# Both heads in one step of a windowed attention, uncast indices and unscaled queries in a routing, and another queue for the gates: one change in four places

## The chip, the cores and the metric

The kernel runs on one core of a Trainium2 chip. The metric is device time in microseconds of one execution; every comparison is between medians of several runs. The engines are TensorE (PE, its weight loads PEld), VectorE (DVE), ScalarE (ACT), GpSimd (POOL) and SyncE (SP, which here issues transfers only).

## The reference

Two transformer-like blocks over 512 tokens of 1024 numbers, in float32, then a norm. The change lies in the second block, which computes (cut):

```
h  = rmsnorm(x);  z = h @ w_in + b_in
conv = silu(layernorm(causal_conv31(val * sigmoid(gate)))) @ w_conv_out
# attention: 16 query heads, 2 key heads, window of 128 keys, one sink per head
m  = maximum(max(s), sink);  e = exp(s - m)
p  = e / (sum(e) + exp(sink - m));  attn = (p @ v) @ w_attn_o
x  = x + (sigmoid(g_conv) * conv + sigmoid(g_attn) * attn) @ w_out
# experts
h2 = rmsnorm(x)
q  = (h2 @ w_pq) in 8 heads of 2 halves;  sc = q . sub_keys      # 128 keys a half
s_top, i_top = top16(sc)                  # for each half
best, pos    = top16(s_top0[:, None] + s_top1[None, :])
idx  = i_top0 * 128 + i_top1 at pos;  gate = softmax(best)       # 128 experts a token
out  = sum over them of gate * gelu(u[idx] . h2) * v[idx]
```

The first block has a stick-breaking attention, a chunked attention, a short convolution and a gated feed-forward part; it is touched by nothing here.

## The kernel before, in words

Features lie on partitions, tokens along the row. Weights come as "units" of 128x1024 numbers, two to a transfer of 1 MB on SP (tile `raw`, two buffers). ScalarE rounds a unit to a high half (`w183h` for unit 183), VectorE or POOL takes the rest as a low half (`w183l`); there are three buffers of each. A product is then three matrix products: high by low, low by high, high by high. `linear` runs a unit's 24 of them into one PSUM tile.

Everything else is a side generator. `Merge` holds lanes (`at` attention, `cv` and `cg` convolution, `ln` norms, `ls` routing, `rw` rows), each with a width, the number of its generators that run at a time. `Clock` models when each engine is free, from sizes only (`cost`): on VectorE 960 elements a microsecond and partition, twice that if all operands are bf16. Ahead of each step of the main stream the generators whose due time has come by the model's TensorE time emit their next step. So a changed modelled cost moves instructions on all engines. `yield ("ls",)` in the main stream runs a lane to its end first.

The stages that matter here, in the order of time:

- Second block's input units with the attention beside them (`swa`, line 865). A generator takes one tile of queries, two heads. It runs four rounds (two pairs of query blocks by two heads): scores into PSUM tiles `w`, their maximum, three operations on the small tile `m` on VectorE, exponentials on ScalarE (`p`), transposes (`pt`), a copy (`pT`), products with the values (`o`), and a multiply by the reciprocal (`oq`).
- The convolution's statistics (`mu`), the layer norm, and its output product `co`.
- Queries of the routing (`pq`), multiplied by the norm's factor (`pqs`), scores (`sk`, copied to `skc`), and `top16` of each 128 (`head_lists`, 16 of them); then for each block of 128 tokens the candidates and their indices (`block_best`), where a one-hot `eq` picks the index.
- 128 units of u (w180 to w307, `u{o}{j}` is unit 180 + 8o + j). Every product of tokens 128 to 511 with all experts is formed, and gelu on ScalarE gives `last`, the activations. For the first 128 tokens rows of u and v are fetched by indirect transfers from POOL (`row`, `last`; four buffers) and VectorE takes the products (a custom instruction, printed as ISA in the order).
- Beside these, for token blocks 1 to 3, `gates`: the chosen indices and gates are transposed (`ijg`, `ijb`); for every 8 tokens VectorE makes five one-hot tiles (`hot`), TensorE multiplies them (`gp`, 24 products of 128x128), ScalarE copies them out (`stage`), and a transfer writes them to `g_dr`. In names such as `hot_3120` the first digit behind `hot` is which of the five, the next the block, the rest the token.
- Behind u15_3 (w303) the lane of the routing is drained and `last_phase` opens new buffers and fetches the gates of the first group of experts (`goct`); behind u15_7 the v units follow (w308 on): `wv` = activation by gate, and products `acc`.

Of the kernel before, what the change touches and what calls it, by code (L numbers as in the profile page):

```python
# [21 lines left out]
P = 128  # L22
# [168 lines left out]
def body(tc, a):  # L191
# [5 lines left out]
    with ExitStack() as ctx:  # L197
# [126 lines left out]
        def t2(name, dt=F32):  # L324
            return wk.tile([P, T], dt, tag="t2", name=name, bufs=NT2)
# [539 lines left out]
        def swa(i):  # L865
            q, k = q2[i], kt2[0]
            oq = t2(f"oq{i}")
            for n, (pr, e) in enumerate(((0, 0), (0, 1), (1, 0), (1, 1))):
                head = 2 * i + e
                if e == 0:  # L870

                    scs = [psd(f"w{i}{n}{x}") for x in range(2)]
                    for sc in scs:
                        PE.matmul(sc, identb, band[:, pr], start=True, stop=False, skip_group_check=True)
                    for b in range(2):
                        qb = 2 * pr + b
                        k0 = max(qb - 1, 0) * P
                        for x, sc in enumerate(scs):
                            rows = slice(x * 64, x * 64 + 64)
                            PE.matmul(sc[:, b * 256 + (P if qb == 0 else 0):(b + 1) * 256],  # L880
                                      q[rows, qb * P:(qb + 1) * P], k[rows, k0:(qb + 1) * P], start=False, stop=True,
                                      skip_group_check=True)
                    sc = None
                sv = scs[e].rearrange("p (b k) -> p b k", b=2)
                scs[e] = None
                m = wk.tile([P, 6, 2], F32, tag="m2", name=f"m2{i}{n}", bufs=8)
                sink = nsk[:, head:head + 1].to_broadcast([P, 2])
                V.tensor_reduce(m[:, 0], sv, axis=AX.X, op=ALU.max, negate=True)

                V.scalar_tensor_tensor(m[:, 1], m[:, 0], 0.125, sink, ALU.mult, ALU.min)  # L890
                V.tensor_tensor(m[:, 2], m[:, 1], sink, ALU.subtract)
                S.activation(m[:, 3], m[:, 2], AF.Exp)
                s = t2(f"p{i}{n}")
                for b in range(2):
                    S.activation(s[:, b * 256:b * 256 + 256], sv[:, b], AF.Exp, scale=0.125, bias=m[:, 1, b:b + 1],
                                 accum_out=m[:, 4, b:b + 1])
                sv = None
                yield at(s)
                V.tensor_tensor(m[:, 5], m[:, 3], m[:, 4], ALU.add)
                V.reciprocal(m[:, 5], m[:, 5])  # L900
                pt = psd(f"pt2{i}{n}")
                c0 = P if pr == 0 else 0
                for c in range(c0 // P, 4):
                    PE.transpose(pt[:, c * P:(c + 1) * P], s[:, c * P:(c + 1) * P], ident)
                pT = t2(f"pT2{i}{n}")
                if e:
                    S.activation(pT[:, c0:], pt[:, c0:], AF.Copy)
                else:
                    V.tensor_copy(pT[:, c0:], pt[:, c0:])
                yield at(pT)  # L910
                o = psd(f"o2{i}{n}")
                for b in range(2):
                    qb = 2 * pr + b
                    cs_ = [c for c in range(2) if qb - 1 + c >= 0]
                    for c in cs_:
                        PE.matmul(o[:, b * 64:(b + 1) * 64], pT[:, (2 * b + c) * P:(2 * b + c + 1) * P],
                                  v2[qb - 1 + c][:, e * 64:(e + 1) * 64], start=c == cs_[0], stop=c == 1)
                V.tensor_tensor(oq.rearrange("p (b e d) -> p b e d", b=NB, e=2)[:, 2 * pr:2 * pr + 2, e],
                                o[:, :P].rearrange("p (b d) -> p b d", b=2),
                                m[:, 5][:, :, None].to_broadcast([P, 2, 64]), ALU.mult)  # L920
# [168 lines left out]
        iota = wk.tile([P, P], F32, name="iota")  # L1089
# [10 lines left out]
        V.tensor_copy(iota16, iota[:, 0:16, None].to_broadcast([P, 16, 16]))  # L1100

# [40 lines left out]
        def block_best(b):  # L1142
# [15 lines left out]
            S.activation(best[:, 1], best[:, 1], AF.Exp)  # L1158
# [5 lines left out]
            far = wk.tile([P, 8, 16], F32, tag="far", name=f"far{b}", bufs=1)  # L1164
            V.tensor_scalar(far, pos[:, 0], float(NC1), None, ALU.is_ge)
# [3 lines left out]
            V.tensor_tensor(d, d, far[:, None].to_broadcast([P, 2, 8, 16]), ALU.mult)  # L1169
# [89 lines left out]
        def peer_u():  # L1259
            mg.spawn("ln", rms_steps(acc, "n4", rr))  # L1260
            for h in range(8):
                qs = []
                for c in range(2):
                    o = yield from linear(hp, f"pq{h}{c}")
                    if h + c == 0:
                        yield ("ln",)
                        mg.spawn("ln", norm2())
                    t = t2(f"pqs{h}{c}")
                    V.tensor_tensor(t, o, rr[1], ALU.mult)
                    qs.append(t)  # L1270
                mg.spawn("ls", head_lists(h, qs))
# [31 lines left out]
        def last_phase():  # L1303
# [8 lines left out]
            h2t.append(wk.tile([P, D], F32, name="h2s"))  # L1312
            S.activation(h2t[1], h2tok, AF.Copy)
            del h2t[0]
            fetch_g(0)

        def fetch_g(n, quarters=range(4)):
            for q in quarters if n < NOCT else ():
# [3 lines left out]
                nc.sync.dma_start(octs[n][:, c], g_dr[VORD[n]][:, c])  # L1322
# [218 lines left out]
```

## Time and profile before

| | |
|---|---|
| median of 3 runs | 2441.09 us (2439.46 to 2441.44) |
| profiled execution | 2439.86 us |
| its span | 2437.8 us |
| mean granted clock of TensorE | 0.988 |
| TensorE, VectorE, ScalarE, POOL busy | 97%, 72%, 42%, 30% |

All compute instructions pass through one helper (line 134), so tiles and not lines tell what an instruction is. The profile leaves out the numbers of tiles in one line's group, so `m` stands for all small tiles of the attention. A row's busy time adds overlapping matrix products once. What an engine waits for is the last releaser of that wait.

### The profile page before, as it was taken

Reading aid. Unit: us, or ns where it says so; the run is one execution under the profiler, and the core shown is the slowest. Engines: PE = TensorE matmul, PEld = TensorE weight load, DVE = VectorE, ACT = ScalarE, POOL = GpSimd, SP = SyncE. Lnnn points to the kernel's source line nnn. Section 1 sums busy time; section 2 is a strip of 40 time slices with the busy share of each in tenths; the row PEclk is TensorE's granted clock in tenths of the full one; section 3 lists DMA queues with packets and bytes.
Section 4 is the critical chain, followed back from the end, with each engine's and each line's share of the span. In section 5 each row is a group of like instructions: output and inputs, shape, how many; then the busy total and the mean of one; then the engine's idle time right before and its main releaser. Section 6 shows DMA issues by size and latency. Waiting matters only on the chain.

```text
span 2437.8 us, 33926 instructions
## 1 busy us (share of the span) xinstructions
PE 2364.7 (97%) x13114; PEld 2111.2 (87%) x13121; DVE 1759.3 (72%) x3167; ACT 1036.0 (42%) x1558; POOL 741.0 (30%) x586
## 2 busy tenths in 40 slices
PE   9999999999999889999999999999998999999997
PEld 7777888888776667777889999999997999999997
DVE  4637644443357789755789898999996888888874
ACT  4454433232246456444324334455554333333333
POOL 2122011110126578401233455333322332323211
PEclk9999999999999999999999999999999999999998
DMA  4110222222211112222224788899998999999972
GB/s 169 57 54 35 91 97 93 104 87 104 87 67 55 52 53 87 87 87 91 93 94 173 292 316 301 313 327 347 345 323 265 360 359 364 353 362 355 372 292 85
DMA packets 141857, 466.14 MB, mean 191 GB/s; under 512 B 10624, under 2 KB 61952, under 8 KB 112000
## 3 DMA queue, kind: packets, MB, share of 16 engines
q1 hardware_dynamic: 52416, 281.04, 31.5%
q0 software_dynamic: 36864, 134.23, 15.5%
q10 hardware_dynamic: 52416, 48.70, 5.9%
q8 instruction: 103, 1.69, 0.3%
q14 instruction: 58, 0.48, 0.1%
HBM read 414.65 MB, written 49.28 MB: 190 GB/s over the span
## 4 chain that ended last, share of the span: by engine, by line
PE 66%; issue 14%; DVE 10%; POOL 4%; ACT 3%; DMA 2%; SPq 0%; POOLq 0%; DVEq 0%; ACTq 0%
PE acc L134 22%; PE u L134 9%; PE up L134 5%; PE gate L134 5%; PE pq L134 3%; PE wo L134 2%; PE qkb L134 2%; DVE hot L134 2%; PE co L134 2%; PE gc L134 2%; POOL row L1054 1%; POOL last L1054 1%; PE ga L134 1%; PE ao L134 1%; DVE cyp L134 1%
## 5 line engine op out<-in xcount | busy, mean ns | idle before, releaser
L134 POOL TENSOR_TENSOR cy<-cy,cvt 128x511 f32<-128x511 f32 (+14 forms) x120 | 173.5, 1445 | 69.7 <-ACT cvt L134 59.1
L134 ACT ACTIVATE last<-u 128x384 f32<-128x384 f32 x128 | 63.0, 492 | 226.1 <-PE u L134 225.9
L1054 POOL DMA_INDIRECT last<-in_un,eid x64 | 80.5, 1257 | 167.9 <-DVE ea L134 131.4
L1054 POOL DMA_INDIRECT last<-in_vn,eid x64 | 70.8, 1106 | 198.9 <-DVE yt L134 188.6
L1054 POOL DMA_INDIRECT row<-in_un,eid x64 | 82.3, 1285 | 136.4 <-DVE ea L134 133.5
L1054 POOL DMA_INDIRECT row<-in_vn,eid x64 | 74.1, 1158 | 153.5 <-DVE yt L134 143.6
L134 ACT ACTIVATE stage<-gp 128x512 f32<-128x512 f32 x96 | 95.9, 1110 | 8.0 <-PE gp L134 8.0
L134 DVE TENSOR_TENSOR hot<-hot,ijb 128x1024 bf16<-128x1024 bf16 x144 | 91.0, 686 | 1.5
L134 PE MATMUL gp<-hot,hot 128*128 128x128 bf16 x1152 | 76.0, 221 | 14.1 <-ACT last L134 6.7
L134 PEld LDWEIGHTS <-hot 128*128 128x128 bf16 x1152 | 67.5, 98 | 24.0 <-DVE hot L134 19.6
L134 DVE SCALAR_TENSOR_TENSOR cyp<-u,par,cyp 128x511 f32<-128x511 f32 (+28 forms) x116 | 85.3, 735 | 2.4
L134 DVE CUSTOM_DVE_ANT_0 last<-last,h2tok 128x1024 f32<-128x1024 f32 x64 | 77.2, 1212 | 10.6 <-DMA last<-in_un,eid 10.6
L134 DVE SCALAR_TENSOR_TENSOR yt<-last,ea,yt 128x1024 f32<-128x1024 f32 x63 | 80.5, 1278 | 2.1 <-DMA last<-in_vn,eid 2.1
L134 DVE SCALAR_TENSOR_TENSOR yt<-row,ea,yt 128x1024 f32<-128x1024 f32 x64 | 81.8, 1278 | 0.1
L134 DVE CUSTOM_DVE_ANT_0 row<-row,h2tok 128x1024 f32<-128x1024 f32 x64 | 77.2, 1213 | 5.7 <-DMA row<-in_un,eid 5.3
L134 ACT ACTIVATE cvt<-u,par 128x511 f32<-128x511 f32 (+14 forms) x120 | 78.9, 700 | 0.0
L134 DVE TENSOR_TENSOR wv<-last,goct 128x384 f32<-128x384 f32 x128 | 70.5, 551 | 0.0
L134 DVE TENSOR_TENSOR hot<-iota,ijb 128x1024 bf16<-128x1024 bf16 x96 | 61.7, 683 | 0.0
L134 DVE TENSOR_TENSOR su<-up,n2r 128x512 f32<-128x512 f32 x22 | 15.2, 691 | 51.8 <-PE up L134 51.8
L134 PEld LDWEIGHTS o<-v,pT 128*128 128x128 f32 x224 | 29.6, 199 | 18.4 <-DVE pT L134 10.9
L134 PE MATMUL o<-v,pT 128*128 128x64 f32 x224 | 31.8, 284 | 10.7 <-DVE pT L134 7.6
L134 DVE MAX8 stop__8676<-skc 128x8 f32<-128x128 f32 x128 | 36.8, 287 | 5.5 <-ACT skc L134 3.2
(6459 smaller groups left out, 8465.9 us busy)
## 6 DMA issues: line engine op xcount, KB each, us to landing
raw<-in_w SPq DMA_DIRECT2D x89, 1024.0 KB, 4.8
raw<-in_u SPq DMA_DIRECT2D x64, 1024.0 KB, 7.4
raw<-in_v SPq DMA_DIRECT2D x64, 1024.0 KB, 7.2
g_dr<-stage ACTq DMA_DIRECT2D x24, 1024.0 KB, 8.4
goct<-g_dr SPq DMA_DIRECT2D x64, 384.0 KB, 8.8
a_dr<-last ACTq DMA_DIRECT2D x14, 1536.0 KB, 9.9
last<-a_dr SPq DMA_DIRECT2D x56, 384.0 KB, 10.3
xT<-in_x_t SPq DMA_DIRECT2D x1, 1024.0 KB, 9.5
```

Source lines behind the costliest of these rows:

```text
L134: return f(*args, **kw)
L1054: nc.gpsimd.indirect_dma_start(row_buf(n), None, t, bass.IndirectOffsetOnAxis(ap=eid[:, n % P:n % P + 1], axis=0))
```

## The change

In `swa` a round takes both heads of the pair: one `m` of 128x6x2x2, one operation on it where two stood, both copies `pT` (one on VectorE, one on ScalarE) in the same round, one multiply into `oq`; the lane `at` is three wide and not four. In the routing the queries are copied by ScalarE without the norm's factor, which goes into the scale of the exponential; the indices stay uint32, without a cast; `far` is computed inside two operations. In the last phase the copy `h2s` is made only if rows of u are left, and `goct` of the first group is issued from POOL's queue and not from SP's.

```
-            for n, (pr, e) in enumerate(((0, 0), (0, 1), (1, 0), (1, 1))):
+            for pr in range(2):
...
-                m = wk.tile([P, 6, 2], F32, tag="m2", name=f"m2{i}{n}", bufs=8)
+                m = wk.tile([P, 6, 2, 2], F32, tag="m2", name=f"m2{i}{pr}", bufs=4)
...
+                V.scalar_tensor_tensor(m[:, 1], m[:, 0], 0.125, sink, ALU.mult, ALU.min)
+                V.tensor_tensor(m[:, 2], m[:, 1], sink, ALU.subtract)
+                ss = [t2(f"p{i}{pr}{e}") for e in range(2)]
+                for e in range(2):
+                    for b in range(2):
+                        c = slice(b * 256, b * 256 + 256)
+                        S.activation(ss[e][:, c], scs[e][:, c], AF.Exp, scale=0.125, bias=m[:, 1, e, b:b + 1],
+                                     accum_out=m[:, 4, e, b:b + 1])
+                S.activation(m[:, 3], m[:, 2], AF.Exp)
+                yield at(*ss)
+                V.tensor_tensor(m[:, 5], m[:, 3], m[:, 4], ALU.add)
+                V.reciprocal(m[:, 5], m[:, 5])
...
+                V.tensor_copy(pT[0][:, c0:], pts[0][:, c0:])
+                S.activation(pT[1][:, c0:], pts[1][:, c0:], AF.Copy)
...
-            mg.width["at"] = 4
+            mg.width["at"] = 3
...
-        itop_ = wk.tile([P, 2, NB, 8, 16], BF16, name="itop_")
-        iu = wk.tile([P, NB, 16], U32, name="iu")
+        itop_ = wk.tile([P, 2, NB, 8, 16], U32, name="itop_")
...
-                    top16(stop_[:, c, b, h], iu[:, b], sc[:, b * P:(b + 1) * P])
+                    top16(stop_[:, c, b, h], itop_[:, c, b, h], sc[:, b * P:(b + 1) * P])
-                V.tensor_copy(itop_[:, c, :, h], iu)
...
-            S.activation(best[:, 1], best[:, 1], AF.Exp)
+            S.activation(best[:, 1], best[:, 1], AF.Exp, scale=rr[0][:, b:b + 1])
...
-            V.tensor_scalar(far, pos[:, 0], float(NC1), None, ALU.is_ge)
-            V.tensor_tensor(d, d, far[:, None].to_broadcast([P, 2, 8, 16]), ALU.mult)
+            for c in range(2):
+                V.scalar_tensor_tensor(d[:, c], pos[:, 0], float(NC1), d[:, c], ALU.is_ge, ALU.mult)
...
-                    V.tensor_tensor(t, o, rr[1], ALU.mult)
+                    S.activation(t, o, AF.Copy)
...
-            fetch_g(0)
+            fetch_g(0, eng=nc.gpsimd)
...
-                nc.sync.dma_start(octs[n][:, c], g_dr[VORD[n]][:, c])
+                eng.dma_start(octs[n][:, c], g_dr[VORD[n]][:, c])
```

The order of instructions moves with it. On TensorE, in the attention behind a product of unit w102, stood before (`pt` transposes, `w` scores, `band` the mask, `o` the product with the values):

```order
L134 MATMUL pt_5059<-ident,p_5033 128x128 x3
L134 LDWEIGHTS identb
L134 MATMUL w_5066<-band,identb 128x512
L134 LDWEIGHTS identb
L134 MATMUL w_5067<-band,identb 128x512
L134 MATMUL w_5066<-k2r,q21r 128x128
L134 MATMUL w_5067<-k2r,q21r 128x128
L134 MATMUL w_5066<-k2r,q21r 128x256
L134 MATMUL w_5067<-k2r,q21r 128x256
L134 MATMUL o_5082<-v_4951,pT_5063 128x64 x3
```

Now stands there, behind the same unit:

```order
L134 MATMUL pt_5076<-ident,p_5033 128x128 x3
L134 MATMUL pt_5077<-ident,p_5034 128x128 x3
L134 LDWEIGHTS identb
L134 MATMUL w_5089<-band,identb 128x512
L134 LDWEIGHTS identb
L134 MATMUL w_5090<-band,identb 128x512
L134 MATMUL w_5089<-k2r,q21r 128x128
L134 MATMUL w_5090<-k2r,q21r 128x128
L134 MATMUL w_5089<-k2r,q21r 128x256
L134 MATMUL w_5090<-k2r,q21r 128x256
L134 MATMUL o_5109<-v_4951,pT_5084 128x64 x3
L134 MATMUL o_5109<-v_4951,pT_5085 128x64 x3
```

The transposes and the products with the values of two heads stand together; before, those of one head.

On TensorE, where the first gate products start, stood before (w254 is u9_2):

```order
L134 MATMUL u_12556<-h2l,w254h 128x384
L134 MATMUL u_12556<-h2h,w254l 128x384
L134 MATMUL u_12556<-h2h,w254h 128x384
L134 LDWEIGHTS hot_10_12467
L134 MATMUL gp_12588<-hot_10_12471,hot_10_12467 128x128
```

And now (w270 is u11_2):

```order
L134 MATMUL u_12939<-h2l,w270h 128x384
L134 MATMUL u_12939<-h2h,w270l 128x384
L134 MATMUL u_12939<-h2h,w270h 128x384
L134 LDWEIGHTS hot_10_12845
L134 MATMUL gp_12966<-hot_10_12849,hot_10_12845 128x128
```

The first gate product has moved behind 16 more units.

On VectorE, at the end of the units of u, stood before (`hot_3120` is the last group of block 3, `ijb` its indices):

```order
L134 TENSOR_TENSOR w305l<-raw_15780,w305h 128x1024
L134 TENSOR_TENSOR hot_3120_16033<-iota_8674,ijb_14930 128x1024
L134 TENSOR_TENSOR hot_3120_16034<-iota_8674,ijb_14930 128x1024
L134 TENSOR_TENSOR hot_3120_16035<-hot_3120_16034,ijb_14930 128x1024
L134 TENSOR_TENSOR hot_3120_16036<-hot_3120_16034,ijb_14930 128x1024
L134 TENSOR_TENSOR hot_3120_16037<-hot_3120_16034,ijb_14930 128x1024
L134 ISA row_9507,ea<-row_9507,h2tok 128x1024
L134 ISA ea 128x1
L134 TENSOR_TENSOR ea<-ea,eg 128x128
L134 TENSOR_TENSOR w306l<-raw_15926,w306h 128x1024
L134 TENSOR_TENSOR w307l<-raw_15926,w307h 128x1024
L134 TENSOR_TENSOR w308l<-raw_16142,w308h 128x1024
```

Now, behind w305l, block 3 starts (`grest`, `ijb`):

```order
L134 TENSOR_TENSOR w305l<-raw_15061,w305h 128x1024
L134 TENSOR_TENSOR grest_15311<-ijg_15306,ijb_15310 128x128
L134 TENSOR_TENSOR ijb_15310<-grest_15311,ijb_15310 128x128
L134 ISA last_9364,ea<-last_9364,h2tok 128x1024
L134 ISA ea 128x1
L134 ISA row_9365,ea<-row_9365,h2tok 128x1024
L134 ISA ea 128x1
L134 TENSOR_TENSOR hot_30_15335<-iota_8546,ijb_15310 128x1024
L134 TENSOR_TENSOR hot_30_15336<-iota_8546,ijb_15310 128x1024
L134 TENSOR_TENSOR hot_30_15337<-hot_30_15336,ijb_15310 128x1024
```

and its last group ends ahead of w306l:

```order
L134 TENSOR_TENSOR hot_3120_15912<-iota_8546,ijb_15310 128x1024
L134 TENSOR_TENSOR hot_3120_15913<-iota_8546,ijb_15310 128x1024
L134 TENSOR_TENSOR hot_3120_15914<-hot_3120_15913,ijb_15310 128x1024
L134 TENSOR_TENSOR hot_3120_15915<-hot_3120_15913,ijb_15310 128x1024
L134 TENSOR_TENSOR hot_3120_15916<-hot_3120_15913,ijb_15310 128x1024
L134 TENSOR_TENSOR w306l<-raw_15207,w306h 128x1024
L134 TENSOR_TENSOR w307l<-raw_15207,w307h 128x1024
L134 TENSOR_TENSOR w308l<-raw_15991,w308h 128x1024
```

Between w305l and w306l there are 80 one-hot tiles and 7 row products now, and 5 tiles and one row product before. On TensorE all 384 products `gp` of block 3 stand between the last product of w303 and the first of w304, where the lane is drained.

## Rows read from the trace of the kernel before

**Rows 1.** Page, part 1: busy time, share of the span, instructions, by engine.
```profile
PE 2364.7 (97%) x13114; PEld 2111.2 (87%) x13121; DVE 1759.3 (72%) x3167; ACT 1036.0 (42%) x1558; POOL 741.0 (30%) x586
```

**Rows 2.** Stretches: length; PE, PEld, DVE, ACT, POOL busy; granted clock; DMA share, GB/s.
```profile
665.70:926.70 261.00, 241.17 (x1210) 184.76 (x1216) 194.14 (x362) 144.12 (x318) 140.81 (x104) 0.97 0.17 61
...
1235.40:1562.40 327.00, 319.73 (x1845) 318.62 (x1844) 294.72 (x888) 126.32 (x171) 156.53 (x95) 0.98 0.70 255
...
1756.30:1860.40 104.10, 96.36 (x794) 92.71 (x793) 99.95 (x153) 54.14 (x67) 34.86 (x27) 0.98 0.96 318
1860.40:1884.20 23.80, 18.73 (x99) 17.84 (x96) 6.11 (x8) 10.58 (x16) 0.00 (x0) 0.93 0.69 237
```

**Rows 3.** Waits of TensorE, 665 to 927: total us, times, longest.
```profile
PE o L134 <- DVE pT L134: 7.6, 8, 2.4
PE pt L134 <- ACT p L134: 4.9, 3, 2.1
```

**Rows 4.** Timeline of VectorE, 812 to 818: start, us, instruction.
```profile
815.42 1.20 DVE L134 TENSOR_TENSOR m<-m 128x2 f32<-128x2 f32 x1
...
816.74 0.54 DVE L134 COPY pT<-pt 128x384 f32<-128x384 f32 x1
```

**Rows 5.** Tile m, 660 to 930: ns min/median/max, first and last start.
```profile
L134 DVE TENSOR_TENSOR m<-m x32: 151/606/1234, 684.3 to 924.6; 128x2 f32<-128x2 f32 x32
```

**Rows 6.** Waits of TensorE, 927 to 1137.
```profile
PE co L134 <- POOL cs7l L134: 2.4, 1, 2.4
PE mu L134 <- DVE s1v L134: 2.3, 1, 2.3
```

**Rows 7.** Waits of TensorE, 1137 to 1562.
```profile
PE u L134 <- ACT w183h L134: 3.3, 1, 3.3
PE u L134 <- POOL w205l L134: 2.2, 1, 2.2
PE u L134 <- POOL w183l L134: 1.7, 1, 1.7
```

**Rows 8.** Timeline of ScalarE, 1236 to 1256 (in brackets idle before, releaser).
```profile
1249.81 0.60 ACT L134 ACTIVATE skc<-sk 128x512 f32<-128x512 f32 x1 [8.62 <-DVE iu L134]
```

**Rows 9.** VectorE's groups by form, 1130 to 1560: busy, mean ns, idle before.
```profile
L134 DVE TENSOR_TENSOR eq<-eq,itop__8677 128x1024 bf16<-128x1024 bf16 x16 | 19.6, 1225 | 0.6
...
L134 DVE TENSOR_TENSOR pqs<-pq,n4r 128x512 f32<-128x512 f32 x16 | 10.9, 682 | 13.2 <-PE sk L134 6.1 <-PE pq L134 4.0 <-ACT n4r L134 3.1
L134 DVE CAST itop__8677<-iu 128x64 bf16<-128x64 uint32 x16 | 8.3, 519 | 0.5
```

**Rows 10.** Timeline of TensorE at two products of u units, w210 and w250.
```profile
1378.95 0.33 PE L134 MATMUL u<-h2l,w210h 128*128 128x384 f32 x1
...
1545.35 0.33 PE L134 MATMUL u<-h2l,w250h 128*128 128x384 f32 x1
```

**Rows 11.** Timeline of VectorE, 1766 to 1783.
```profile
1766.89 1.29 DVE L134 TENSOR_TENSOR hot<-iota,ijb 128x1024 bf16<-128x1024 bf16 x2
...
1777.46 1.21 DVE L134 CUSTOM_DVE_ANT_0 last<-last,h2tok 128x1024 f32<-128x1024 f32 x1
...
1778.60 1.28 DVE L134 TENSOR_TENSOR hot<-iota,ijb 128x1024 bf16<-128x1024 bf16 x2
...
1781.73 1.22 DVE L134 TENSOR_TENSOR w293l<-raw,w293h 128x1024 fp32r<-128x1024 f32 x1
```

**Rows 12.** Chain of waits, 1855 to 1886: start, us, what.
```profile
1859.71 3.59 ACT stage L134 x4
...
1863.32 5.06 DMA g_dr<-stage
...
1870.25 7.60 DMA raw<-in_v
...
1880.12 0.56 DVE wv L134
```

**Rows 13.** Page, part 5: row fetches on POOL, busy us and mean ns.
```profile
L1054 POOL DMA_INDIRECT row<-in_vn,eid x64 | 74.1, 1158 | 153.5 <-DVE yt L134 143.6
```

More of the change, by code (lines that the diff above doesn't have):

```diff
@@ L867, in swa @@
             oq = t2(f"oq{i}")
-            for n, (pr, e) in enumerate(((0, 0), (0, 1), (1, 0), (1, 1))):
[L869 to L874, printed above, removed]
+            sink = nsk[:, 2 * i:2 * i + 2, None].to_broadcast([P, 2, 2])
+            for pr in range(2):
+                scs = [psd(f"w{i}{pr}{e}") for e in range(2)]
+                for sc in scs:
+                    PE.matmul(sc, identb, band[:, pr], start=True, stop=False, skip_group_check=True)
+                for b in range(2):
+                    qb = 2 * pr + b
+                    k0 = max(qb - 1, 0) * P
+                    for e, sc in enumerate(scs):
+                        rows = slice(e * 64, e * 64 + 64)
+                        PE.matmul(sc[:, b * 256 + (P if qb == 0 else 0):(b + 1) * 256],
+                                  q[rows, qb * P:(qb + 1) * P], k[rows, k0:(qb + 1) * P], start=False, stop=True,
+                                  skip_group_check=True)
+                m = wk.tile([P, 6, 2, 2], F32, tag="m2", name=f"m2{i}{pr}", bufs=4)
+                for e in range(2):
+                    V.tensor_reduce(m[:, 0, e], scs[e].rearrange("p (b k) -> p b k", b=2), axis=AX.X, op=ALU.max,
+                                    negate=True)
+                V.scalar_tensor_tensor(m[:, 1], m[:, 0], 0.125, sink, ALU.mult, ALU.min)
+                V.tensor_tensor(m[:, 2], m[:, 1], sink, ALU.subtract)
+                ss = [t2(f"p{i}{pr}{e}") for e in range(2)]
+                for e in range(2):
+                    for b in range(2):
+                        c = slice(b * 256, b * 256 + 256)
+                        S.activation(ss[e][:, c], scs[e][:, c], AF.Exp, scale=0.125, bias=m[:, 1, e, b:b + 1],
+                                     accum_out=m[:, 4, e, b:b + 1])
+                S.activation(m[:, 3], m[:, 2], AF.Exp)
+                scs = sc = None
+                yield at(*ss)
+                V.tensor_tensor(m[:, 5], m[:, 3], m[:, 4], ALU.add)
+                V.reciprocal(m[:, 5], m[:, 5])
+                pts = [psd(f"pt2{i}{pr}{e}") for e in range(2)]
+                c0 = P if pr == 0 else 0
+                for e in range(2):
+                    for c in range(c0 // P, 4):
+                        PE.transpose(pts[e][:, c * P:(c + 1) * P], ss[e][:, c * P:(c + 1) * P], ident)
+                pT = [t2(f"pT2{i}{pr}{e}") for e in range(2)]
+                V.tensor_copy(pT[0][:, c0:], pts[0][:, c0:])
+                S.activation(pT[1][:, c0:], pts[1][:, c0:], AF.Copy)
+                ss = pts = None
+                yield at(*pT)
+                o = psd(f"o2{i}{pr}")
+                for e in range(2):
@@ L875, in swa @@
                     for b in range(2):
                         qb = 2 * pr + b
[L877 to L882, printed above, removed]
@@ L892, in swa @@
[L892 to L901, printed above, removed]
@@ L902, in swa @@
[L902 to L917, printed above, removed]
@@ L918, in swa @@
-                V.tensor_tensor(oq.rearrange("p (b e d) -> p b e d", b=NB, e=2)[:, 2 * pr:2 * pr + 2, e],
-                                o[:, :P].rearrange("p (b d) -> p b d", b=2),
-                                m[:, 5][:, :, None].to_broadcast([P, 2, 64]), ALU.mult)
+                        cs_ = [c for c in range(2) if qb - 1 + c >= 0]
+                        for c in cs_:
+                            PE.matmul(o[:, (2 * b + e) * 64:(2 * b + e + 1) * 64],
+                                      pT[e][:, (2 * b + c) * P:(2 * b + c + 1) * P],
+                                      v2[qb - 1 + c][:, e * 64:(e + 1) * 64], start=c == cs_[0], stop=c == 1)
@@ L1088, in u_rows @@
                 yield due
-        iota = wk.tile([P, P], F32, name="iota")
+        iota = t2("iota")[:, :P]
         G.iota(iota, pattern=[[1, P]], base=0, channel_multiplier=0, allow_small_or_imprecise_dtypes=True)
@@ L1100, in body @@
         V.tensor_copy(iota16, iota[:, 0:16, None].to_broadcast([P, 16, 16]))
+        iota = None
         def top16(vals, idx, x):
@@ L1311, in last_phase, with fetch_g @@
             yts.append(wk.tile([P, D], F32, name="yt"))
-            h2t.append(wk.tile([P, D], F32, name="h2s"))
-            S.activation(h2t[1], h2tok, AF.Copy)
-            del h2t[0]
-            fetch_g(0)
-        def fetch_g(n, quarters=range(4)):
+            if rows[0] < P:
+                h2t.append(wk.tile([P, D], F32, name="h2s"))
+                S.activation(h2t[1], h2tok, AF.Copy)
+                del h2t[0]
+            fetch_g(0, eng=nc.gpsimd)
+        def fetch_g(n, quarters=range(4), eng=nc.sync):
             for q in quarters if n < NOCT else ():
```

12 lines of the change are left out of this document (4 added, 8 removed).

## The prediction

> **What bounds the kernel now.** I read five views, from the whole to the single wait. The page's first part shows TensorE busy for 97% of the span [rows 1], so only three things can move the end: TensorE's idle stretches, the clock it is granted, and work added to it. The order holds the same matrix products before and after, so the third is out. The stretches by stage [rows 2] then say where the idle time is. In the attention stage of block 2 (665.7 to 926.7) TensorE idles 261.0 − 241.2 = 19.8 us; in the stretch of the lists and the first expert units (1235.4 to 1562.4) 7.3 us; in the third block of gates (1756.3 to 1860.4) VectorE is busy for 99.95 of 104.1 us, so that it is the bound there and TensorE waits for it; and in the turn from u to v (1860.4 to 1884.2) TensorE idles 5.1 us and its clock is 0.93. The waits of TensorE [rows 3, 6, 7] name what it waits for, the timelines [rows 4, 8, 11] show why that was late, and the chain of waits [rows 12] gives the turn.
>
> What I decide by is the last of these stretches but one. A unit of u alone takes TensorE (1545.35 − 1378.95) / 40 = 4.16 us [rows 10]. In the third block of gates 17 units (w287 to w303) take 104.1 us, 6.1 us each: there VectorE makes five one-hot tiles, one low half of a weight and about one row product for each unit. Beside the units this costs 2 us a unit; by itself, without a unit beside it, it would cost the whole of VectorE's time.
>
> **The change part by part.**
>
> *The gates come 16 units later.* The order shows it on two engines. The first one-hot product stands behind w270, where it stood behind w254. The first two blocks keep their units (w270 to w303), but for the third no unit is left to go beside: the main stream asks at that place for the lane to be drained, and all 80 one-hot tiles of the third block run on VectorE between w305l and w306l, with TensorE at work on nothing but the gate products that hang on them. The price comes from two pieces. (a) Sixteen units that had gates beside them go without: 16 × 4.16 = 66.6 us, bound by TensorE. VectorE has in them 17 low halves and 17 row products at about 1.14 us each (38.8 us), ten one-hot tiles (6.3) and four sets of work on eq (0.64 us as for a one-hot tile, 1.23 us, and four smaller sums, an estimate of 3 us a set), together some 57 us [rows 9, 11], so it keeps up. (b) The third block alone. Before, its first unit starts at 1756.3 and its first one-hot tile at 1766.9 [rows 11]: 10.6 us, which come again. A group of five tiles lasts from 1778.60 to 1781.73, so 3.13 us; 16 groups are 50.1 us. Seven row products stand among them in the order, at 1777.46 to 1778.60 = 1.14 us each: 8.0 us. The last gate product and its copy: some 1.8 us (half of the four copies of 3.59 in [rows 12]). Together 70.5 us. Before, all this took 104.1 us. So 66.6 + 70.5 − 104.1 = **+33 us**. The ends: +25, if the head's 10.6 us (in it three row products with waits for their rows) shrink to 3; +36, if two more row products wait some 1.5 us each for a row that comes late.
>
> *The turn.* Before: the copies, 5.06 us for the gates to be written out, four issues of goct on SP (1868.4 to 1870.2), and behind them on the same queue the weights of the first v unit, 7.60 us, which the chain followed to the end [rows 12]. Now goct is issued from POOL's queue; SP's queue is clear, so the weights arrive beside the tail and drop out of the chain. In their place stands goct itself: the copies to 1863.3, 5.06 us, four issues at no more than the 1.16 us of a POOL row fetch [rows 13], a landing between 5.06 and 7.60 us (the two transfers of [rows 12], for 384 KB instead of 1024), and from the first wv to the first product of v 1884.2 − 1880.1 = 4.1 us. That is 21.7 to 24.3 us against 23.8. I take −2, ends −6 (four short issues, a landing of 3 us) and +2. The row fetches stand ahead of goct on POOL, three of them; they wait for row products that are done by then. The copy of h2 that is left out (ScalarE) is off this path, worth nothing. The tail's products come with gaps, and the clock that such a stretch is granted is 0.98 to 0.93 in [rows 2]; for the start of v at half clock I add +1 (0 to +3).
>
> The Trainium skill, "DMA: Bandwidth & Descriptors", sections "Specifications" and "Issuing engine by pattern", speaks against the move: a plain load belongs on Sync, since the first byte of a DMA issued from GpSimd comes after about 1 us instead of 0.6. By its figures the turn would be an estimated 0.4 us longer than I say; no row of before shows a plain load on that queue, and the sum does without it.
>
> *The second attention.* Both heads of a step share their small operations: one sum, one reciprocal, one multiply by it instead of two. The one that hurts is the sum of exponentials: 128x2 elements, yet 0.15 us at the least, 0.61 in the median and 1.23 at the most, 32 times [rows 5]. At 815.42 one takes 1.20 us, and the copy of pT that TensorE needs stands behind it on VectorE [rows 4]; TensorE's waits for pT, eight in all, come to 7.6 us [rows 3]. With 16 of these sums instead of 32 half of that goes, −3.8. Against it: the transposes now wait for four exponentials instead of two, and the order packs a pair's products closer together, 17 steps of the main stream where 31 stood. That can double the wait for p, 4.9 us. What can be won at all is the idle 19.8 us and the clock, 3% of 261 = 7.8 us: 27.6 us. I take a third of it, **−9**, since the busier half of its waits is the one that is halved; ends −20 (nearly three quarters of it) and +5 (the wait for p doubled).
>
> The row [rows 5] gives no reason for its 1.23 us. The Trainium skill, "SBUF — State Buffer", section "SBUF: two separate sides", has one: a VectorE operation with two inputs in SBUF and a GpSimd operation that reads SBUF take turns at one port pair, for a whole instruction each. By that rule the shared sum waits as long as the single one and only their number counts, half of them gone; by the row read as a plain duration it would be the same half, but a doubled operand would cost a little more. The trace agrees in size (a minimum of 0.15 and a maximum of 1.23), and the sum is the same by both to 1 us.
>
> *The layer norm and the convolution's output.* The statistics' product comes 11 steps earlier in the order than before. Before, TensorE waits 2.3 us there, and the output's products wait 2.4 us for their normed inputs [rows 6]; with more steps between, the latter goes, the former shrinks by half, and some clock comes with it, half a microsecond: **−4**, ends −7 and 0 (its inputs are ready no earlier, as the additions of the convolution on POOL set them).
>
> *The routing.* Sixteen multiplies of queries (682 ns, idle before them 13.2 us) and sixteen casts (519 ns) leave VectorE [rows 9]; the copies on ScalarE cost about the 0.60 us of an skc copy [rows 8] and lie beside TensorE's work. Each list leaves VectorE 0.68 + 0.52 = 1.2 us sooner. That matters at one place: the copy of scores at 1249.81 waited 8.62 us for the lists [rows 8], the high half w183h stood behind it on ScalarE, and TensorE waited 3.3 us for it and 1.7 us for its low half; further on 2.2 us for w205l, which stands behind row fetches on POOL and now goes to VectorE [rows 7]. After seven lists the gain is 8 us, more than the 5 us that were missing. So 3.3 + 1.7 + 2.2 = 7.2 us, and some 1.8 of the clock, which the stretch shows at 0.98: **−9**, ends −13 (all of the clock's 2%) and −2. The multiply of eq with uncast indices runs at 1225 ns already [rows 9], the rate of the fp32 low half (1.22) and not of bf16 one-hot tiles (half of 1.28); I cost it at 0, ends −2 and +4, but the planner prices it higher now, which is part of why the gates come late. The two operations for `far` become two of about the same size: 0. All this is VectorE's time under units that TensorE bounds; if that cover were gone it would be 16 × 1.2 = 19 us gained.
>
> **The sum**, against the profiled execution of 2439.86 us (the median of the runs, 2441.09, is 1.2 us higher): +33 − 2 + 1 − 9 − 4 − 9 = +10, so 2449.9, given as 2450 us.
>
> **The rivals.** 0.2%, 4.9 us, is about what a measurement of this kernel can tell from no change.
>
> *Faster.* The attention's, the convolution's and the lists' stalls all go, with the clock's share: −20 − 7 − 13 = −40 against +32: 2432 us. It decides from 37 us of stalls won. For it: these stalls are in few places and the order loosens each; against it: nothing in the order shortens the exponentials' path, and the wait for p may grow. Chance 0.18.
>
> *Level.* 27 to 36 us of stalls are won, or the tail costs 25 and the stalls give 20 to 29: 2436 to 2446. Chance 0.26.
>
> *My forecast*, the tail of about 30 us and stalls of 12 to 27 us: 2446 to 2458. Chance 0.41.
>
> *A denser attention stalls more.* Three heads' pairs in flight with two chains of exponentials each, where TensorE has nothing between: +5 there, and the lists' and convolution's gains at their low ends: 33 − 1 + 5 − 0 − 2 = +35, 2475; with half of their gains 2465. Chance 0.12.
>
> *The third block is not alone after all*: if the one-hot tiles ran so far ahead of their products that w304 to w307 hid 4 × 4.16 = 16.6 us of them, 2433. The order places them behind w303 on both engines, and a tile has two buffers at most: chance 0.03, on the faster side.
>
> Faster 0.18 + 0.03 = 0.21, level 0.26, slower 0.41 + 0.12 = 0.53. The range that leaves out about a tenth on either side is 2433 to 2465; the forecast's own is 2443 to 2458.
>
> **What would show it.** Right: between the last product of w303 and the first of w304 some 70 us with TensorE busy for half of it and VectorE full of one-hot tiles; units w254 to w269 at 4.2 us each; no wait for w183h; waits for pT under 5 us in the attention stage, its window 5 to 12 us shorter; goct, not raw, last before the first v product. Wrong: one-hot tiles between u units to the end, a stretch from w287 to w304 of less than 90 us, or an attention stage shorter by over 20 us, which would give the faster case.

## The result, and the profile after

The changed kernel takes 2469.84 us (2465.43 to 2471.86, 4 runs) against 2440.4 us: a ratio of 1.0121, 95% interval [1.0109, 1.0134]. It is slower by 29 us, 1.2%; the forecast was 2450 us with a range to 2465. The profiled execution took 2470.82 us, its span is 2468.8 us, 31.0 us more than before.

By stretches of the same units of work (columns as in [rows 2]), these of the changed kernel answer to those of before: attention, w180 to w199, the 16 units that go without gates, the third gates block, and the turn.

```profile
669.70:935.90 266.20, 248.97 (x1222) 188.37 (x1221) 192.15 (x299) 145.36 (x307) 144.01 (x107) 0.94 0.16 58
1239.20:1342.90 103.70, 95.20 (x546) 93.47 (x545) 82.02 (x392) 39.75 (x55) 45.23 (x19) 0.97 0.38 135
1567.50:1634.40 66.90, 66.90 (x389) 66.86 (x388) 56.18 (x86) 24.10 (x34) 20.27 (x18) 1.00 0.86 315
1824.30:1893.60 69.30, 33.56 (x411) 30.38 (x409) 63.67 (x105) 32.41 (x37) 11.28 (x10) 0.83 0.70 224
1893.60:1915.10 21.50, 16.96 (x101) 16.64 (x98) 6.24 (x8) 8.50 (x13) 3.24 (x5) 0.97 0.60 213
```

The third and fourth row are the forecast's tail: 66.9 us without gates (66.6 said), then one block of gates by itself, 69.3 us (70.5 said) with TensorE busy for less than half and VectorE for 92%. The first two rows are where the forecast went wrong: the attention was to become 9 us shorter and is 266.2 us long against 261.0 [rows 2], and the first 20 units of u take 103.7 us against 97.9, in the row of before:

```profile
1235.40:1333.30 97.90, 92.84 (x546) 92.09 (x545) 86.74 (x399) 37.63 (x52) 42.93 (x18) 0.97 0.42 146
```

The waits of TensorE in the attention (total us, times, longest):

```profile
PE o L134 <- DVE pT L134: 9.1, 7, 2.3
PE pt L134 <- ACT p L134: 3.9, 3, 2.4
```

The same from w180 to w199:

```profile
PE u L134 <- POOL w183l L134: 2.0, 1, 2.0
PE u L134 <- POOL w181l L134: 2.0, 1, 2.0
PE u L134 <- POOL w182l L134: 2.0, 1, 2.0
PE u L134 <- ACT w182h L134: 0.9, 1, 0.9
PE u L134 <- ACT w181h L134: 0.8, 1, 0.8
PE u L134 <- ACT w183h L134: 0.8, 1, 0.8
```

And between the start of w303 and that of w304:

```profile
PE gp L134 <- DVE hot L134: 35.7, 16, 10.2
```

Against [rows 3] the wait for pT has not halved but grown. Against [rows 7] the one late unit w183 has become three late units, 8.5 us instead of 5.0 (3.3 + 1.7), while the wait for w205l is gone.

Why units are late is seen on ScalarE, changed kernel, 1222 to 1262 (in brackets the idle time before, and its releaser):

```profile
1235.91 0.60 ACT L134 ACTIVATE skc<-sk 128x512 f32<-128x512 f32 x1 [0.60 <-PE sk L134]
1243.64 0.60 ACT L134 ACTIVATE pqs<-pq 128x512 f32<-128x512 f32 x1 [7.13 <-DVE itop__8549 L134]
1244.13 1.05 ACT L134 ACTIVATE w181h<-raw 128x1024 fp32r<-128x1024 f32 x1
...
1252.80 0.60 ACT L134 ACTIVATE pqs<-pq 128x512 f32<-128x512 f32 x1 [7.13 <-DVE itop__8549 L134]
1253.29 1.05 ACT L134 ACTIVATE w182h<-raw 128x1024 fp32r<-128x1024 f32 x1
```

A copy of queries takes 0.60 us, but ahead of it ScalarE stands idle for 7.13 us until a list on VectorE (`itop`) is through: the copy needs a buffer that the list frees. The high half of the next weight unit stands behind the copy. That holds for w181 and w182; w183h stands behind a copy of scores (`skc` at 1259.40) that waited 5.07 us for TensorE, which the two late units had held up.

And in the attention, the timeline of VectorE, 895 to 903:

```profile
899.07 1.44 DVE L134 TENSOR_TENSOR w127l<-raw,w127h 128x1024 fp32r<-128x1024 f32 x1 [2.17 <-ACT w127h L134]
900.43 1.20 DVE L134 TENSOR_TENSOR m<-m 128x4 f32<-128x4 f32 x1
901.66 0.18 DVE L134 RECIPROCAL m<-m 128x4 f32<-128x4 f32 x1
901.76 0.53 DVE L134 COPY pT<-pt 128x384 f32<-128x384 f32 x1
```

On POOL ran at that time:

```profile
899.79 1.82 POOL L134 TENSOR_TENSOR cy<-cy,cvt 128x503 f32<-128x503 f32 x1 [0.36 <-ACT cvt L134]
```

The shared sum still takes 1.20 us, and it ends (901.63) when POOL's addition ends (901.61). Ahead of it VectorE waits 2.17 us for a high half on ScalarE, and that half stands there behind the round's four exponentials (the fourth of them, and the half):

```profile
896.83 0.48 ACT L134 ACTIVATE p<-w,m 128x256 f32<-128x256 f32 x1
897.98 1.06 ACT L134 ACTIVATE w127h<-raw 128x1024 fp32r<-128x1024 f32 x1
```

A sum of 1.20 us is the exception now. All sums of the stage, before (first row) and after: busy time, mean ns, idle before.

```profile
L134 DVE TENSOR_TENSOR m<-m 128x2 f32<-128x2 f32 x32 | 19.9, 622 | 1.5 <-ACT p L134 1.5
L134 DVE TENSOR_TENSOR m<-m 128x4 f32<-128x4 f32 x16 | 7.8, 487 | 1.2 <-ACT m L134 1.2
```

So the sums fell from 19.9 to 7.8 us, and the wait for pT grew all the same. In all seven waits VectorE had itself waited 1.1 to 2.2 us just ahead of the sum and the copy, for a high half (of a weight or of the attention's output) that stands on ScalarE behind four exponentials; before, it had waited for one in two of eight. In five of the seven the sum takes 0.15 to 0.30 us, as in this one, where TensorE waits 1.3 us for the copy:

```profile
691.86 1.22 DVE L134 TENSOR_TENSOR w105l<-raw,w105h 128x1024 fp32r<-128x1024 f32 x1 [1.09 <-ACT w105h L134]
693.01 0.15 DVE L134 TENSOR_TENSOR m<-m 128x4 f32<-128x4 f32 x1
693.29 0.53 DVE L134 COPY pT<-pt 128x384 f32<-128x384 f32 x1
```

### The profile page after: what moved, and what is told of

The parts are those of the page before. It is cut to its first block, busy times and chain, and to the rows that moved or that the text cites. A ratio compares the mean times of both kernels' runs of the same rounds, so it can differ in the third digit from the quotient of the medians.

```text
span 2468.8 us, 33841 instructions
## 1 busy us (share of the span) xinstructions
PE 2375.5 (96%) x13121; PEld 2120.1 (86%) x13121; DVE 1734.9 (70%) x3057; ACT 1041.5 (42%) x1557; POOL 722.4 (29%) x588
## 4 chain that ended last, share of the span: by engine, by line
PE 71%; issue 14%; DVE 7%; POOL 4%; ACT 3%; DMA 1%; SPq 0%; POOLq 0%; DVEq 0%; ACTq 0%
PE acc L134 22%; PE u L134 14%; PE up L134 5%; PE gate L134 5%; PE pq L134 3%; DVE hot L134 2%; PE wo L134 2%; PE qkb L134 2%; PE co L134 2%; PE ao L134 2%; PE gc L134 2%; POOL row L1056 1%; PE g L134 1%; POOL last L1056 1%; DVE m L134 1%
## 5 line engine op out<-in xcount | busy, mean ns | idle before, releaser
L1056 POOL DMA_INDIRECT row<-in_un,eid x64 | 74.0, 1156 | 150.8 <-DVE ea L134 147.9
L134 ACT ACTIVATE p<-w,m 128x256 f32<-128x256 f32 x64 | 29.4, 472 | 36.5 <-DVE m L134 33.3
```

What stands on the lines that cost most here:

```text
L134: return f(*args, **kw)
L1056: nc.gpsimd.indirect_dma_start(row_buf(n), None, t, bass.IndirectOffsetOnAxis(ap=eid[:, n % P:n % P + 1], axis=0))
```

## The experiments

Times are medians, and so are differences of totals in us. The ratios, with 95% intervals, are to the kernel before, run on the same chip; they differ by up to 0.1% from the quotient of the two medians.

**The attention alone, taken out and put in.** e1 puts the old `swa` (and width 4) into the changed kernel; e2 puts the new one (and width 3) into the kernel before.

> The changed kernel with the attention of before (one head a round, four wide); the rest as changed. Theory: the attention's new form costs the 5 us by which its stage is longer in the profile (266.2 against 261.0), so about 2465 us, stage near 261, the third gates block still alone behind w303. Rival, clock by chance: the 5 us are half-clock stretches that fall anywhere, then 2467 to 2472 and some other stage has them. Rival, the attention's new order is what puts the gates late: then 2440.

> The kernel before with only the attention in its new form, three wide. Theory: attention stage near 266 instead of 261, total 2440 + 5 = 2445; gates still from w254 on. Rival, clock by chance: 2438 to 2442, since idle time in the stage fell by 2 us. Rival, attention puts the gates late: 2468.

Measured: e1 2470.24 us, 1.0132 [1.0115, 1.0149], as the whole change. e2 2438.6 us, 0.9998 [0.9988, 1.0007]. The new attention is worth nothing in the total, and it is not what puts the gates late. But chance is not the whole reason either. In six profiles with the old form (before, e1, e7, e8, e9, e15) the attention stage takes 258.5 to 261.0 us, in eight with the new one (after, e2, e3, e5, e6, e10, e14, e16) 261.8 to 266.2: about 3 us longer. The stretch behind it, to w164, takes 209.5 to 210.8 with the old and 204.7 to 207.8 with the new: about 4 us shorter. The two stretches of e2:

```profile
664.89:927.74 262.85, 244.21 (x1214) 187.06 (x1220) 192.33 (x298) 145.34 (x307) 145.16 (x106) 0.95 0.16 57
927.74:1132.47 204.73, 200.43 (x879) 163.70 (x878) 141.26 (x170) 99.63 (x139) 71.35 (x49) 1.00 0.26 91
```

Idle time of the attention is 18.6 us there, against 19.8 in [rows 2]; what grew is TensorE's busy time, 244.2 against 241.2 us, at a granted clock of 0.95 instead of 0.97.

**The planner's price.** e3 prices each VectorE operation by its output's type, so that the multiply of eq has its old price (and a few small operations that turn wider inputs into bf16 a lower one than before); e7 puts the new price into the kernel before and changes nothing else.

```
# e3, in the changed kernel
-            two = all(x.dtype == BF16 for x in (out, *ins))
+            two = out.dtype == BF16
# e7, in the kernel before
-            two = all(x.dtype == BF16 for x in (out, *ins))
+            two = all(x.dtype == BF16 for x in (out, *ins)) and not (name == 'tensor_tensor' and 'itop' in ins[-1].tensor.name)
```

> The changed kernel, but the planner prices a VectorE operation by its output's type alone, so that the multiply of eq with uint32 indices is priced like a bf16 one, as before the change (0.60 instead of 1.14 us, 16 times); no operation changes. Theory: the gates start behind w254 again, the stretch from w254 to w304 is near 298 us instead of 326, total 2470 - 28 = 2442. Rival, the late gates are hidden or repaid elsewhere: over 2460. Rival, VectorE cannot keep the earlier place since the uint32 multiply is slower in truth: the stalls come back between w235 and w254, 2450 to 2460.

> The kernel before, not one operation changed, but the planner prices the multiply of eq with the indices at 960 elements a microsecond (1.14 us, near the 1.225 us that it takes) instead of 1920. Theory: this alone moves the gates behind w270 and leaves the third block alone behind w303, so the stretch from w254 to w304 is near 326 us and the total 2440 + 28 = 2468. Rival, in the kernel before the moved lists fill the units that go without gates, and less is lost: 2450 to 2460.

Measured: e3 2450.82 us, 1.0056 [1.0039, 1.0073]; e7 2461.76 us, 1.0103 [1.0083, 1.0123]. With one price of the planner changed and not one operation, the kernel before loses 23 us by medians (25 by the ratio). Its stretches of 16 units without gates and of the third block:

```profile
1558.20:1625.10 66.90, 66.90 (x389) 66.86 (x388) 55.13 (x85) 23.98 (x34) 19.61 (x17) 1.00 0.86 311
1816.50:1885.00 68.50, 31.61 (x409) 28.52 (x408) 63.71 (x105) 32.11 (x37) 12.17 (x11) 0.88 0.70 218
```

They are the changed kernel's two rows again. Some of the loss comes back before them: w200 to w254 takes 224.6 us in e7 and 229.1 before, half of it the wait for w205l, which is gone with the other order, and the rest TensorE's busy time at a full clock (224.64 us, granted clock 1.00, against 226.87 at 0.99). The price is the nearer one to the truth (1.14 us against a measured 1225 ns, with bf16 indices in [rows 9] and with uint32 indices here), and it makes the worse order.

```profile
L134 DVE TENSOR_TENSOR eq<-eq,itop__8549 128x1024 bf16<-128x1024 bf16 x13 | 15.9, 1225 | 0.4
```

e3 gets back 19 us and not 28. The stretch from w254 to w304 takes 306.3 us and not 298, since one more group of gate products is left behind w303 (17.6 us there instead of 13.1) and the units ahead of it are slower; and w200 to w254 takes 228.1 us again.

**The copies of queries.** e5 puts them back on VectorE in the changed kernel (without the factor); e9 puts them on ScalarE in the kernel before.

```
# e5
-                    S.activation(t, o, AF.Copy)
+                    V.tensor_copy(t, o)
# e9, with the factor in the exponential's scale
-                    V.tensor_tensor(t, o, rr[1], ALU.mult)
+                    S.activation(t, o, AF.Copy)
```

> The changed kernel with the 16 copies of queries on VectorE instead of ScalarE. Theory: on ScalarE each copy waits for a buffer that VectorE's lists free, and the high halves w181h to w183h wait behind it (9.4 us of TensorE's waits); on VectorE the waits for w181 and w182 go and the one for w183 comes back (5 us): total 2470 - 3 = 2467. Rival, VectorE's lists themselves are late: the waits are as long as before or longer, 2470 to 2478.

> The kernel before with only the queries changed: copied by ScalarE without the factor, which goes into the exponential. Theory: the copies wait for buffers that VectorE's lists free, the high halves w181h to w183h wait behind them: the stretch from w180 to w190 is near 60 us instead of 54, total 2440 + 6 = 2446. Rival, ScalarE has room and VectorE's lists get 0.68 us shorter each: 2435 to 2440.

Measured: e5 2460.23 us, 1.0085 [1.0069, 1.0102]; e9 2447.57 us, 1.0033 [1.0021, 1.0045]. So the copies on ScalarE cost 8 to 10 us, where I had expected 3 and 6. In e9's profile w180 to w199 takes 103.5 us (97.9 before) and w200 to w253 takes 233.0 (229.1). The longest waits of TensorE in e9 from w180 to w253:

```profile
PE u L134 <- POOL w205l L134: 4.3, 1, 4.3
PE u L134 <- POOL w181l L134: 2.0, 1, 2.0
PE u L134 <- POOL w183l L134: 2.0, 1, 2.0
PE u L134 <- POOL w182l L134: 2.0, 1, 2.0
PE u L134 <- ACT w182h L134: 0.9, 1, 0.9
PE u L134 <- ACT w181h L134: 0.8, 1, 0.8
```

Five are those of the changed kernel; the first is that of [rows 7], twice as long. In e5 only the old pair for w183 is left, 3.3 and 1.7 us.

**More buffers for them.** e10 gives the routing 11 buffers instead of 7 and pays with one of the two buffers of `stage`; e14 to e16 make room by going back to bf16 indices with a cast, and have 8.

```
# e10
-        NT2 = 7
+        NT2 = 11
# e14: 8, and
+        itop_ = wk.tile([P, 2, NB, 8, 16], BF16, name="itop_")
+        iu = wk.tile([P, NB, 16], U32, name="iu")
...
+                    top16(stop_[:, c, b, h], iu[:, b], sc[:, b * P:(b + 1) * P])
+                V.tensor_copy(itop_[:, c, :, h], iu)
# e15 and e16: as e14, copies as in e5; e15 with the old attention
```

> The changed kernel with 11 instead of 7 buffers for the queries and scores of the routing; for the room the gates' stage has one buffer instead of two, so only the stretch from w180 to w200 is read. Theory: the copies of queries on ScalarE wait for buffers that VectorE's lists free; with four more they go ahead, and so do w181h to w183h: 98 us or less instead of 103.7, idle 5 us or less instead of 8.5. Rival, the time of the copies on ScalarE, or the lists on VectorE, hold the high halves: 103 us again.

> The changed kernel with bf16 indices and their cast, as before, and in the room this gives 8 instead of 7 buffers for queries and scores; the copies of queries stay on ScalarE. Theory: the gates start behind w254 again, and one buffer more lets the copies go ahead: the stretch from w180 to w200 is under 98 us (103.7 with 7 buffers), total 2470 - 28 - 6 = 2436. Rival, one buffer is not enough, or the copies' own time on ScalarE counts: 103 us, total 2442 to 2446.

> As e14, with the query copies on VectorE and the attention of before, so of the change only the goct queue, far, iota's place and the factor in the exponential are left, and 8 buffers. Theory: 2434.6 of e8 minus the waits for w183 that the buffer takes away, 5 us: 2430. Rival, nothing waits for buffers when VectorE makes the copies: 2434 to 2437.

> As e15, with the attention's new form. Theory: the new form is worth nothing in the total (its stage 3 us longer, the convolution's 4 us shorter): within 2 us of e15. Rival, it is worth its 5 to 9 us on either side once the rest is out of the way: e15 plus or minus 5 or more.

e10, w180 to w199, in one profile:

```profile
1229.82:1320.28 90.46, 90.46 (x545) 90.45 (x544) 76.14 (x360) 37.97 (x52) 43.18 (x18) 1.00 0.44 152
```

90.5 us instead of 103.7, no idle time at all and a full clock: with the buffers there, the copies' own time on ScalarE counts for nothing. (e15 and e16, with the copies on VectorE and 8 buffers, have the same 90.5 us.) Its total, 2525.9 us in its only run, says nothing of the copies: w254 to w304, with one stage buffer for the gates, takes 398.0 us. e14 measures 2430.26 us, 0.9956 [0.9938, 0.9974]; with 8 buffers the stretch is 91.9 us, though the cast is back on VectorE, where e9, with the cast and 7, takes 103.5:

```profile
1234.34:1326.20 91.86, 90.75 (x545) 90.42 (x544) 81.41 (x376) 37.51 (x52) 44.38 (x19) 1.00 0.44 152
```

On ScalarE the copies still wait in e14, but sooner: w181h begins 2.1 us ahead of w180's first product (1234.34), where in the changed kernel it begins 4.9 us behind it (1244.13 and 1239.2). Of the three units only w182 is late, by 1.1 us:

```profile
1231.78 0.60 ACT L134 ACTIVATE pqs<-pq 128x512 f32<-128x512 f32 x1 [7.15 <-DVE iu L134]
1232.27 1.05 ACT L134 ACTIVATE w181h<-raw 128x1024 fp32r<-128x1024 f32 x1
```

e15 measures 2431.46 us, 0.9969 [0.9958, 0.9981], e16 2431.69 us, 0.9966 [0.9955, 0.9976]: the old and the new attention are level once nothing else is in the way, and with one more buffer no difference was measured between copies on ScalarE (e14) and on VectorE (e16).

**The queue of goct.** e8 is the kernel before with `fetch_g(0, eng=nc.gpsimd)`.

> The kernel before with only the first goct issued from POOL's queue (the copy h2s stays). Theory: the weights of the first v unit no longer stand behind goct on SP; the turn from w304 to w308 shrinks from 23.8 to about 21.5 us: 2438, which is within 0.2%. Rival, the page's rule that loads from GpSimd start later decides: 24 us or more, 2440 to 2442.

Measured: 2434.64 us, 0.9986 [0.9976, 0.9996], and a turn of 21.1 us against 23.8. In the changed kernel's chain the turn goes like this (start, us, what):

```profile
1900.93 0.59 POOL goct L1324
...
1901.52 1.11 POOL goct L1324 x2
1902.62 7.97 DMA goct<-g_dr
...
1910.97 0.57 DVE wv L134
...
1915.08 2.93 PE acc L134 x7
```

The weights of v are out of the chain, as forecast. An issue takes 0.55 to 0.59 us, half of the 1.16 that bounded it; the landing takes 7.97, more than the 7.60 that bounded it from above (6.24 in e8).

**Both causes taken out together.** e6 has the price of e3 and the copies of e5.

> The changed kernel with the lower price of e3 and the query copies on VectorE of e5. Theory: the two causes are the whole loss and add up: 2470 - 19 - 9 = 2442, within 0.2% of before. Rival, both take from the same VectorE time, so that the second gives little once the first is done: 2449 to 2452.

Measured: 2442.84 us, 1.0017 [1.0004, 1.0029]. The two add up.

**Gates still earlier.** e11, e12 and e13 make VectorE cheaper in the planner (`n / (1920 if two else 1050)`; e12 with 2400 for bf16), the first two on e8, the third on e6.

> The kernel before with goct on POOL's queue and a planner that takes VectorE at 1050 instead of 960 elements a microsecond, so that the gates start 4 units earlier and no gate product is left behind w303. Theory: where the third block ends in the units of u, its tail of 13.1 us becomes a common 6: 2434.6 - 7 = 2428. Rival, VectorE is the bound of the whole stretch and pays elsewhere what it saves: 2433 to 2437.

> As e11, with bf16 operations at 2400 elements a microsecond as well: gates from w246 to w287, 8 units earlier than before. Theory: the gates use VectorE's free time ahead of w254, but a unit with gates takes longer and one without takes 4.16 us whichever comes first: 2426 to 2432, close to e11. Rival, one-hot tiles too early hold up the lists and the low halves: 2440 or more.

> The changed kernel with the query copies on VectorE, the lower price of the index multiply and VectorE at 1050 elements a microsecond, gates from w250 to w298. Theory: as e6 (2443) without the tail of 17 us behind w303: 2432, since the turn is 2 us shorter than before and no more is lost. Rival, the new attention's extra half-clock time stays and it ends at 2436 to 2440.

Measured: 2452.28 us, 1.0054 [1.004, 1.0067]; 2469.18 us, 1.0121 [1.0105, 1.0136]; 2443.24 us, 1.0019 [1.0009, 1.0029]. My theories fell for all three. The tail did go as forecast: in all three w303 takes 4.2 us (13.1 in e8, 17.2 in e6) and the turn 17.4 (21.1 and 21.3). But the number reaches every stage: the first block, from w4 to w98, takes 624.8 and 626.2 us in e11 and e12 instead of 616.4 before, its idle time 6.8 instead of 1.9; e13 loses 8.9 us against e6 up to w98. And gates that start earlier do not come cheaper as a whole. From w235 to w304 e12 takes 402.5 us where before takes 377.45; this is e12:

```profile
1496.90:1899.40 402.50, 364.97 (x2819) 350.54 (x2818) 349.51 (x527) 197.37 (x243) 106.75 (x95) 1.00 0.89 309
1498.00:1825.00 327.00, 291.47 (x2381) 277.94 (x2382) 318.21 (x494) 168.75 (x205) 99.31 (x86) 1.00 0.94 327
```

TensorE waited for one-hot tiles 37 times, 34.8 us in all. The second row is about w235 to w286 of it: VectorE is the bound there, busy for 318.2 of 327.0 us. In the rest, 75.5 us, it is busy for 31.3 us, so its work and TensorE's lie less beside each other than before.

## Why the prediction was wrong

*The gates' tail*, +33, was right in mechanism and near in size: from w254 to w304, before and after, +28.

```profile
1562.35:1860.40 298.05, 282.77 (x2359) 272.13 (x2359) 286.35 (x435) 164.67 (x199) 97.50 (x73) 0.99 0.96 327
1567.50:1893.60 326.10, 286.17 (x2363) 276.64 (x2362) 305.08 (x470) 167.03 (x203) 94.05 (x74) 0.96 0.89 306
```

The pieces were 66.9 (66.6 said) and 69.3 (70.5 said); the rest is that the first two blocks cost 189.9 us beside w270 to w302 and had cost 193.9 beside w254 to w286. e7 shows the price as the cause of it, by itself, and e3 the way back.

*The turn*, −2, was right as a sum: −2.3 in the profile, −2.7 in e8's. Its pieces offset each other, which is luck: the issues in the chain took 1.7 us where four of 1.16 were allowed, the landing more than its bound. And not all of it is the queue's: in e7, with goct still on SP, the turn takes 22.3 us. The +1 for the clock did not come; the granted clock of the turn was 0.97 against 0.93. That the Trainium skill's page "DMA: Bandwidth & Descriptors" (section "Issuing engine by pattern") puts plain loads on Sync did not decide: e8, with plain loads on POOL's queue, is faster than before; a later start of the landing was not measured by itself.

*The convolution's output*, −4, was right: the stretch to w164 is 5.1 us shorter in the profile, about 4 over all of them. The wait for `mu`, though, did not shrink (2.9 us against 2.3); what went is the wait for `cs7l` and half-clock time.

*The second attention*, −9, is the first step that failed. The argument was that half of the small sums would take half of the waits for pT. The sums did shrink, from 19.9 to 7.8 us, and the waits went from 7.6 to 9.1 us (8.6 in e2, 8.9 in e16). What holds the copy now is VectorE's own wait for a high half, which stands on ScalarE behind four exponentials in a row. The prediction had those four against it, but only for the wait for p, and that one fell (3.9 us against 4.9). No run moves the high halves, so this is read from the traces and not shown by an experiment. The dear sums are explained: all 21 of over 0.2 us before, and all 8 after, end within 0.02 us of an instruction on POOL, as the Trainium skill's page "SBUF — State Buffer" (section "SBUF: two separate sides") has it. With the clock the stage is about 3 us longer over eight profiles. Why the new form gets more half-clock time, with less idle time, was not settled.

*The routing*, −9, is the second. I had seen on ScalarE that a copy of scores waited 8.62 us for the lists with a high half behind it [rows 8], and added 16 copies to that same queue, with buffers from the same ring, at nothing. Four of the last five brought a wait of 4.8 to 7.1 us for VectorE's lists to the engine that feeds TensorE. The stretch to w199 grew by 5.8 us instead of shrinking; e9 has the loss at 8.9 us in all. e10 takes it away in that stretch by buffers alone, e14 with one more buffer and the cast back. (The multiply of eq was costed at 0 rightly, but [rows 9] shows it with cast indices and not, as the prediction reads it, with uncast ones; the row of the changed kernel above does.) The 2.2 us of w205l in that step's sum did come, but from the order that the price makes: the wait is gone in e7 and still there in e9.

*What the sum left out*: in the first block, where the order of TensorE is the same as before, the profile after is 4.3 us longer. It has a piece at half clock there with TensorE busy throughout, the second row of this fence (the first is w20 to w23 whole; before, that took 51.9 us, the last row):

```profile
187.50:243.70 56.20, 55.60 (x285) 41.84 (x284) 37.51 (x89) 26.84 (x61) 13.22 (x17) 0.91 0.11 38
196.90:207.10 10.20, 10.20 (x40) 6.97 (x39) 3.95 (x10) 5.39 (x16) 0.49 (x2) 0.50 0.00 0
187.80:239.70 51.90, 51.24 (x286) 38.62 (x283) 36.56 (x89) 26.39 (x61) 13.27 (x17) 1.00 0.11 41
```

Three of the 14 profiles with that order have it (after, e5, e8), whatever was changed further on; so 4 of the 31 us between the two profiled executions are no part of the change. What brings it about stays open.

Step by step, each in the kernel before: price +23, copies +9, attention −0.6, queue −4, by medians 27 of the 29 us. The ratios give 1.0103 × 1.0033 × 0.9998 × 0.9986 = 1.0120 against 1.0121 for all together, which is closer than their intervals warrant. `far`, the missing copy `h2s` and the missing cast were in no run by themselves. The three steps that were to win 22 us came to −0.6 (e2, for attention and convolution) and +9 (e9, for the routing).

The rival of the denser attention named 2475 us, nearer to 2470 than the forecast, but by luck: it counted on no gain at the convolution and 2 at the lists, where 4 were won and 9 lost.

e8 beats both kernels by a little (0.9986); the fastest versions are e14 to e16, which their intervals do not tell apart. The nearest to the change is e14: the change without the uncast indices, and their room given to one more buffer.

## What to carry to other kernels

A move of an operation to a less busy engine moves its waits too: ask what buffer it needs, who frees it, and what stands behind it on the new queue. Where a planner lays out the order, a changed operand type is a changed price; compare the order before the time, and treat a better price as a change of its own. An operation in front of a late one can become cheaper without making it earlier: ask what else stands ahead of it on its engine, and what that waits for.

## What the runs showed of the hardware that was not expected

A multiply of bf16 by bf16 and one of bf16 by uint32, both 128x1024 into bf16, took the same 1225 ns; the cast bought nothing in that operation, as the prediction had costed it. An issue of a plain load on POOL's queue took 0.55 to 0.59 us, where an indirect row fetch takes 1.16. And a stretch of 10.2 us at a granted clock of 0.50, the level of 1.2 GHz, came in the middle of unbroken TensorE work (busy throughout from 180.0 us to its start at 196.9), in 3 of 14 profiles, worth 4 to 5 us each time.
